# A hybrid encoder layer on one core: operands of the second half's input projection from x with channels on partitions

## The chip, the cores and the metric

The kernel runs on one core of a Trainium2 chip. The core has a matrix engine (TensorE, PE), three engines for element-wise work (VectorE or DVE, ScalarE or ACT, GpSimd or POOL), a queue engine that only issues transfers (SyncE, SP), and 16 DMA engines between the chip's memory and the on-chip SBUF. TensorE adds its products up in PSUM. The metric is the device time of one execution in microseconds; less is better. Several executions were timed, and one more was recorded by the hardware profiler.

## The reference

One layer with 2048 tokens and 1024 channels, all in float32. Cut to what matters here:

```python
xn = rmsnorm(x, norm1_g[l])          # x * rsqrt(mean(x*x) + 1e-6) * g
z = xn @ w_in[l]                     # the input projection, all columns
...
merged = gates[:, :, 0] * ya + gates[:, :, 1] * yb
x = x + merged @ w_o[l]
x = x + conv_glu_ffn(rmsnorm(x, norm2_g[l]), w_up[l], conv_w[l], conv_b[l], w_down[l])
...
return rmsnorm(x, final_g)
```

The change concerns the first two lines for the second half of the tokens: the normalised x is wanted with channels on partitions, since the matrix engine contracts over partitions.

## The kernel before

**Numbers.** A float32 operand is split into a high and a low part that the matrix engine takes at full rate (`split`, L680: the high part by ScalarE, L686, or GpSimd, L684; the low part, source minus high, by VectorE, L687). A product takes three matmuls of 128x512: high by high, high by low, low by high (`n_step`, L700).

**Seven products.** Large products run as a Strassen-like scheme: operands are cut into 2x2 blocks, and seven products P1 to P7 of sums of blocks replace eight. For x, the blocks are channels 0-511 or 512-1023 (four tiles of 128 channels each, k = 0..3 and 4..7) of one block of 512 tokens or the next: B11 and B21 from the first block, B12 and B22 from the second. The sums are T1 = B12 - B11, T2 = B22 - T1, T3 = B22 - B12 and T4 = B21 - T2 (up to the sign that the code keeps B22 with). Names such as `x_T20h` are the high part of T2, tile 0; `x_f0h` to `x_f7h` are those of B11 and B21.

**Stages.** The tokens are done in two halves of 1024, each of two blocks `b` of 512 (first half 0 and 1, second half 2 and 3); a block has four row tiles `j` of 128 tokens. Each half runs `mixer` and then `ffn`. `mixer` begins with `proj_io` (L1320), whose products come in the order P1, P2, P6, P5, ..., into the PSUM banks io_X, io_Y, io_Z, io_V: io_X uses B11, io_Y uses B21, the first io_Z uses T2, and io_V uses T1. `ffn` ends with the down-projection `down` (banks dn_P, L154 on PE as all matmuls with weights), in the order P1, P6, P2, P7, P5, P4, P3, each of 11 steps: a step takes one tile of weights and does 12 matmuls, three for each of four row tiles. So the end of the first half is dn P4, dn P3, and then the second half's io_X, io_Y, io_Z, io_V.

**Weights.** SP loads each tile of weights (`raw`, eight buffers, L203); ScalarE makes the high part (L250) and VectorE the low part (L251) in a ring of six (`ops`).

**Order.** Other work is written as tasks (generators) that are advanced a step every few matmuls; from what has been emitted, the framework's scheduler arranges the instructions by its own estimates, and each engine then runs its own list strictly in order. Working tiles come from one pool of 73 SBUF slots of 128x512 (`slot`).

**The forms of x, before.** `forms_of` (L935) makes two tasks. `forms_a_task` (L770) and `forms_b_task` (L819) first run `norm_rows` (L734) on the row tiles (`load_rows` loads them with tokens on partitions): ScalarE squares and sums a row (L727), GpSimd makes the root 1/sqrt(mean + eps) of each token (L730, L731), and VectorE scales the rows with it (`x_xs`, L744). TensorE then transposes 128x128 pieces into PSUM (`x_t`, L750), and ScalarE copies them out, times the gain (`x_b`, L758; with the sign turned, L850). The sums T1, T2, T3 are VectorE instructions that read PSUM (`minus`, L839), T4 is L891. For the second half, `forms_of` is called in `each3`, at step k = 1 (`X_AT`) of dn P3; the rows were loaded in dn P4 (`each4`). `go_io` keeps the second task from going on to transposes until `mixer` sets it.

**Beside it.** After dn P4 and dn P3 the first half's result gets its last normalisation (`final`): square sums `fj` on ScalarE (L1794), root on GpSimd (`fss`, L1852; `f_0r` and so on, L720 and L721), products `fo` on VectorE (L1861) or on ScalarE and GpSimd (L1858, L1859), and out. GpSimd's queue also fetches the operands of dn (`g_P`, L998), and SP loads `fg`, the last gain as one row for all partitions (L1900).

Of the kernel before, what the change touches and what calls it, by code (L numbers as in the profile page):

```python
# [11 lines left out]
F32 = mybir.dt.float32  # L12
F32R = mybir.dt.float32r
U8 = mybir.dt.uint8
AF = mybir.ActivationFunctionType
ALU = mybir.AluOpType
AX = mybir.AxisListType

P = 128
SEQ = 2048  # L20
D = 1024
KD = D // P
# [6 lines left out]
EPS = 1e-6  # L29
TB = 512  # L30
NT = TB // P
# [32 lines left out]
N_HEADS = 2  # L64
GO_AT = 3
LEAD = 5
X_AT = 1
WARM = 24, 5
GO_IO = (("P2", 1), ("P2", 0))
G_POOL = 4  # L70
# [11 lines left out]
LOOKAHEAD = 4  # L82
# [4 lines left out]
def tile_trunk(  # L87
    ctx: ExitStack,
    tc: tile.TileContext,
    x: bass.AP,  # L90
    w_in_t: bass.AP,
    w_io: bass.AP,
    pool_wt: bass.AP,
# [21 lines left out]
    def slot(name, cols=TB, dt=F32):  # L115
        return slots.tile([P, cols], dt, tag="s", name=name, padded_shape=[P, 528])
# [183 lines left out]
    stream = Stream()  # L300
# [271 lines left out]
    xt = {}  # L572
    ready = set()
# [9 lines left out]
    def load_rows(b):  # L583
        for j in range(NT):
            load_x_tile(b, j)
# [23 lines left out]
    def col(o):  # L609
        return cols[:, o : o + 1]  # L610
# [123 lines left out]
    def norm_rows(src, name, xs, after, lag=1):  # L734
        for j in range(NT):
# [9 lines left out]
                xs[j, hf] = t[hf]  # L745
            after(j)

    def transpose(ps, xs, j, k):
        c = (k % 4) * P
        return pe.transpose(ps[:, j * P : (j + 1) * P], xs[j, k // 4][:, c : c + P], ident)  # L750
# [184 lines left out]
    def forms_of(kind, b, gain, after=lambda b: lambda j: None, early=False, go=lambda: True):  # L935
        forms = {k: [] for k in ("B11", "B21", "B22", "T1", "T2", "T3", "T4", "task")}
        full = {k: [] for k in ("B11", "B21", "T2")}
        first = Task(forms_a_task((kind, b), gain, forms, full, after(b), early))
        forms["task"].append(first)
        late = Task(forms_b_task((kind, b + 1), gain, forms, full, after(b + 1), go, early))  # L940
        return forms, first, late

    def need(forms, key, late):
        task = forms["task"][0] if key in ("B11", "B21") else late
# [761 lines left out]
    def ffn(b0, forms, late):  # L1706
# [202 lines left out]
        def each3(k):  # L1909
            if k == 0:  # L1910
                down.make(len(down.steps))
            if k == X_AT and not last:
                nxt.append(forms_of("x", b0 + 2, o_n1, go=lambda: go_io[0]))

        def each4(k):
            if k in (0, 4) and not last:
                load_rows(b0 + 2 + k // 4)

        flush()
        down.run("P1", 0, each0)  # L1920
# [1 line left out]
        down.run("P2", 0, each1)  # L1922
        down.run("P7")
        down.run("P5", 0, each2)
        down.run("P4", 2, each4, lambda j: Task(final(0, j)))
        go_io[0] = False
        down.run("P3", 5 if last else 3, each3, lambda j: Task(final(1, j)), last)
        return nxt[0] if nxt else None

# [71 lines left out]
```

## Time and profile before

| | before |
|---|---|
| median of 3 timed executions | 2472.25 us (2472.08 to 2472.85) |
| the profiled execution | 2470.74 us |
| its span in the trace | 2468.7 us |
| granted TensorE clock | 1.0 |
| HBM traffic | 232 GB/s over the span |

The span is what the trace covers from the first to the last instruction; the execution's own time is 2 us longer. The page's rows with the most to do with the change are quoted in the prediction. Busy time is how long an engine worked; the chain of work that ended last is followed back from the last instruction, and says which engine's work set the end. A group's row gives the instructions of one line with their tiles, their count, busy time, mean length of one in ns, and how long the engine had idled before them. In the row of a window the brackets give the number of instructions.

### The profile page before, as it was taken

The numbers are of one execution on the slowest core, as the hardware profiler recorded it, in microseconds if no ns is written. First come the engines' busy times: TensorE is split into PE (matmuls) and PEld (weight loads), VectorE is DVE, ScalarE is ACT, GpSimd is POOL, SyncE is SP. The second block draws the span as 40 slices with busy tenths as digits, with TensorE's granted clock in tenths as the row PEclk, the third lists the DMA queues.
The fourth block names the chain that finished last, engine by engine and source line by source line (L and its number), as shares of the span: only waits on it lengthen the run. The fifth ranks groups of instructions, "written<-read, shape, count | busy, mean of one in ns | idle before, by whom it ended". The sixth has DMA issues, their size and how long they took to land.

```text
span 2468.7 us, 37997 instructions
## 1 busy us (share of the span) xinstructions
PE 2448.3 (99%) x12708; PEld 1986.6 (80%) x12708; DVE 1921.2 (78%) x3318; ACT 1237.0 (50%) x2376; POOL 783.6 (32%) x1090
## 2 busy tenths in 40 slices
PE   9999999999999999999999999999999999999998
PEld 7887877788888888888888888887888888888887
DVE  7777776897998778875586667769889987778755
ACT  6545544435555454553555455552465544445534
POOL 5343353403444333551330101123033332335310
PEclk9999999999999999999999999999999999999999
DMA  8889887777898779897444343456343444447852
GB/s 271 271 223 270 246 220 232 244 229 251 205 264 232 224 224 246 269 357 241 137 149 151 128 134 124 150 191 236 124 137 126 152 154 136 145 144 252 312 167 98
DMA packets 257699, 497.83 MB, mean 202 GB/s; under 512 B 26912, under 2 KB 47520, under 8 KB 257184
## 3 DMA queue, kind: packets, MB, share of 16 engines
q1 hardware_dynamic: 189872, 317.53, 38.9%
q0 software_dynamic: 42656, 112.74, 17.9%
q10 hardware_dynamic: 24976, 65.13, 7.6%
q8 instruction: 100, 1.64, 0.3%
q14 instruction: 95, 0.78, 0.1%
HBM read 383.63 MB, written 189.27 MB: 232 GB/s over the span
## 4 chain that ended last, share of the span: by engine, by line
PE 91%; DVE 4%; DMA 1%; issue 1%; ACT 1%; POOL 0%; SPq 0%; ACTq 0%; DVEq 0%; POOLq 0%
PE dn_P L154 17%; PE up_Z L154 15%; PE up_V L154 10%; PE up_X L154 10%; PE wo_P L154 6%; PE gr_V L154 3%; PE gr_X L154 3%; PE pb L154 3%; PE io_Z L154 3%; PE io_V L154 2%; PE gr_Z L154 2%; PE fr_V L154 1%; PE gr_W L154 1%; PE fr_X L154 1%; PE gr_Y L154 1%
## 5 line engine op out<-in xcount | busy, mean ns | idle before, releaser
L250 ACT CAST ops<-raw 128x512 fp32r<-128x512 f32 x792 | 487.1, 620 | 784.2 <-PE dn_P L154 175.2
L251 DVE TENSOR_TENSOR ops<-raw,ops 128x512 fp32r<-128x512 f32 x792 | 590.1, 749 | 238.8 <-ACT ops L250 226.6
L1735 DVE SCALAR_TENSOR_TENSOR e<-h,cols,e 128x512 f32<-128x512 f32 x176 | 143.0, 817 | 30.1 <-ACT e L1733 25.5
L1733 ACT ACTIVATE e<-h,cols 128x512 f32<-128x512 f32 x176 | 142.2, 814 | 25.2 <-DVE h L1183 18.7
L998 POOL DMA_DIRECT2D g_P<-dg_P x154 | 83.7, 545 | 173.7 <-PE dn_P L154 125.5
L1738 DVE SCALAR_TENSOR_TENSOR e<-h,cols,e 128x512 f32<-128x512 f32 x176 | 133.9, 770 | 2.5
L1304 POOL TENSOR_TENSOR gf_P<-e,e 128x512 f32<-128x512 f32 x44 | 61.6, 1402 | 149.4 <-DVE e L1744 89.4
L472 POOL TENSOR_TENSOR raw<-raw,raw 128x512 f32<-128x512 f32 x36 | 52.2, 1451 | 99.0 <-DVE ops L251 72.3
L1304 POOL TENSOR_TENSOR gf_P<-gf_P,e 128x512 f32<-128x512 f32 x44 | 58.4, 1328 | 74.0 <-DVE e L1744 71.7
L1728 POOL COPY h<-h 128x2 f32<-128x2 f32 x88 | 40.0, 466 | 107.3 <-DVE h L1182 99.6
L1742 ACT ACTIVATE e<-e 128x512 f32<-128x512 f32 x88 | 55.6, 632 | 35.1 <-DVE e L1738 34.8
L1183 DVE TENSOR_TENSOR h<-up_u,up_V 128x512 f32<-128x512 f32 x88 | 60.1, 683 | 10.4 <-PE up_V L154 9.9
L1730 POOL COPY hist<-h 128x2 f32<-128x2 f32 x88 | 35.2, 401 | 99.1 <-DVE h L1183 97.0
L1728 POOL COPY h<-hist 128x2 f32<-128x2 f32 x88 | 46.9, 539 | 53.8 <-ACT ops L250 35.5
L1444 POOL TENSOR_TENSOR q<-q,qs 128x512 f32<-128x512 f32 x16 | 22.3, 1397 | 122.2 <-ACT qs L1443 122.2
L1279 DVE TENSOR_TENSOR x<-x,wo_P 128x512 f32<-128x512 f32 x88 | 55.9, 681 | 6.2 <-PE wo_P L154 6.0
L1279 DVE TENSOR_TENSOR ac<-ac,dn_P 128x512 f32<-128x512 f32 x72 | 47.2, 681 | 12.3 <-PE dn_P L154 11.9
L1223 ACT COPY up_e<-up_X 128x512 f32<-128x512 f32 x44 | 25.8, 587 | 60.6 <-PE up_X L154 39.0
L1477 ACT ACTIVATE gt<-gt,cols 128x512 f32<-128x512 f32 x48 | 34.8, 725 | 42.1 <-DVE gt L1183 41.0
L1758 POOL DMA_DIRECT2D dg_P<-gf_P x88 | 50.7, 576 | 8.2 <-POOL gf_P L1304 7.4
L720 POOL TENSOR_SCALAR ro<-so 128x4 f32<-128x4 f32 x16 | 3.9, 244 | 147.6 <-ACT sq L1156 147.3
L1618 POOL TENSOR_TENSOR ya<-ya,gl 128x512 f32<-128x512 f32 x24 | 36.7, 1552 | 26.1 <-DVE ya L1615 17.6
(1326 smaller groups left out, 7916.1 us busy)
## 6 DMA issues: line engine op xcount, KB each, us to landing
g_P<-dg_P POOLq DMA_DIRECT2D x154, 256.0 KB, 5.7
raw<-in_w_up_t SPq DMA_DIRECT2D x132, 256.0 KB, 3.1
raw<-in_w_in_t SPq DMA_DIRECT2D x98, 256.0 KB, 3.6
dg_P<-gf_P POOLq DMA_DIRECT2D x88, 256.0 KB, 3.8
dg_P<-e SPq DMA_DIRECT2D x66, 256.0 KB, 3.3
raw<-in_w_dn SPq DMA_DIRECT2D x66, 256.0 KB, 3.6
x<-in_x SPq DMA_DIRECT2D x64, 256.0 KB, 4.8
gd<-gt ACTq DMA_DIRECT2D x64, 256.0 KB, 3.6
```

The source lines that it names most:

```text
L154: count[1] = pe.matmul(*args, **kw)
L250: self.mark = act.copy(hi, v)
L251: low = self.low = dve.tensor_tensor(lo, v, f32(hi), ALU.subtract)
L998: eng.dma_start(t, d)
L1183: return dve.tensor_tensor(dst, t, ps, ALU.add if how == "add" else ALU.subtract)
L1279: dve.tensor_tensor(t, t, ps[j], ALU.add if sg > 0 else ALU.subtract)
L1304: pin(eng.tensor_tensor(t, x0, x1, op))
L1728: pool.tensor_copy(h[:, 0:2], hist[:, mt] if hf == 0 else hs[s, 0][:, TB : TB + 2])
L1733: in_turn(act.activation(t, h[:, 2:], AF.Identity, bias=col(o_cb + mt), scale=col(o_cw + 4 * MF + mt)))
L1735: in_turn(second(dve.scalar_tensor_tensor(t, h[:, 1 : 1 + TB], col(o_cw + 2 * MF + mt), t, ALU.mult, ALU.add)))
L1738: dve.scalar_tensor_tensor(t, h[:, 0:TB], col(o_cw + mt), t, ALU.mult, ALU.add)
L1742: in_turn(act.activation(g, g, AF.Silu))
```

## The change

The kernel gets x a second time, as `x_ct`, its transpose: 1024 channels by 2048 tokens, laid out so on the host before the launch. For the second half (blocks 2 and 3) `channel_forms` replaces `forms_of("x", ...)`. A tile of channels is loaded as it stands (`xc`). Squares of the rows are still summed on ScalarE from the row tiles, but the four sums of a block become one 128x4 root on GpSimd, which is written to DRAM (`rx`, 512 elements of 4 bytes) and read back as one row of 512 tokens broadcast to all partitions (`x_rt`). `normed` is one VectorE instruction: channel tile times gain (one per partition) times root. The sums T1 to T4 are VectorE instructions on SBUF tiles. The tasks are now made at step 8 of dn P4 and not at step 1 of dn P3, and `go_io` is cleared before dn P4. The first half, and the forms of the up-projection, stay as they were.

```diff
-X_AT = 1
+X_AT = 8
...
+    def load_channels(b, k):
+        t = slot(f"xc{b}_{k}")
+        sp.dma_start(t, x_ct[k * P : (k + 1) * P, b * TB : (b + 1) * TB])
+        return t
+
+    def root_rows(b, name):
+        ss = small.tile([P, 2, 4], F32, tag="ssx", name=f"{name}ss")
+        for j in range(NT):
+            while (("x", b), j) not in ready:
+                yield 1
+            for c in range(2):
+                act.activation(slot(f"{name}xs{j}_{c}"), xt.pop((("x", b), j, c)), AF.Square,
+                               scale=1.0 / 32.0, accum_out=ss[:, c, j : j + 1])
+        r = small.tile([P, 4], F32, tag="rstd", name=f"{name}r")
+        pool.tensor_tensor(r, ss[:, 0], ss[:, 1], ALU.add)
+        pool.tensor_scalar(r, r, 1.0, EPS, ALU.mult, ALU.add)
+        pool.tensor_tensor(r, r, neghalf, ALU.pow)
+        d = dram.tile([NT, P], F32, tag=f"rx{b}", name=f"rx{b}")
+        pool.dma_start(d.rearrange("j p -> p j"), r)
+        t = slot(f"{name}rt")
+        pool.dma_start(t, d.rearrange("j p -> (j p)").partition_broadcast(P))
+        return t
+
+    def normed(xc, rt, c, name):
+        t = slot(name)
+        dve.scalar_tensor_tensor(t, xc, c, rt, ALU.mult, ALU.mult)
+        return t
+
+    def channels_a_task(b, gain, forms, full):
+        name = f"x{b}_"
+        xc = [load_channels(b, k) for k in range(4)]
+        rt = yield from root_rows(b, name)
+        yield 4
+        for k in range(KD):
+            key = "B11" if k < 4 else "B21"
+            t = normed(xc[k], rt, col(gain + k), f"{name}b{k}")
+            if k + 4 < KD:
+                xc.append(load_channels(b, k + 4))
+            yield 1
+            full[key].append(t)
+            forms[key].append(split(t, f"{name}f{k}", True))
+
+    def channels_b_task(b, gain, forms, full, go):
+        name = f"x{b}_"
+        xc = [load_channels(b, k) for k in (0, 4)]
+        rt = yield from root_rows(b, name)
+        yield 6
+        b12, b22, t1 = [], [], []
+        for k in range(4):
+            x12, x22 = xc[2 * k : 2 * k + 2]
+            if k < 3:
+                xc += [load_channels(b, i) for i in (k + 1, k + 5)]
+            b12.append(normed(x12, rt, col(gain + k), f"{name}c{k}"))
+            b22.append(normed(x22, rt, negs[:, gain + k + 4 : gain + k + 5], f"{name}b{k}"))
+            yield 3
+        while not go() or len(full["B21"]) < 4:
+            yield 1
+        for k in range(4):
+            t1.append(slot(f"{name}t1{k}"))
+            dve.tensor_tensor(t1[k], b12[k], full["B11"][k], ALU.subtract)
+            t2 = slot(f"{name}t2{k}")
+            dve.scalar_tensor_tensor(t2, b22[k], -1.0, t1[k], ALU.mult, ALU.subtract)
+            forms["T2"].append(split(t2, f"{name}T2{k}"))
+            full["T2"].append(t2)
+            yield 1
+        for k in range(4):
+            forms["T1"].append(split(t1[k], f"{name}T1{k}"))
+            yield 4
+        for k in range(4):
+            dve.tensor_tensor(b12[k], b12[k], b22[k], ALU.add)
+            forms["T3"].append(split(b12[k], f"{name}T3{k}"))
+            yield 1
+        for k in range(4):
+            t4 = slot(f"{name}t4{k}")
+            dve.tensor_tensor(t4, full["B21"][k], full["T2"][k], ALU.subtract)
+            forms["T4"].append(split(t4, f"{name}T4{k}"))
+            forms["B22"].append(split(b22[k], f"{name}B22{k}"))
+            yield 1
+        stream.room = LOOKAHEAD
...
+    def channel_forms(b, gain, go):
+        forms = {k: [] for k in ("B11", "B21", "B22", "T1", "T2", "T3", "T4", "task")}
+        full = {k: [] for k in ("B11", "B21", "T2")}
+        first = Task(channels_a_task(b, gain, forms, full))
+        forms["task"].append(first)
+        return forms, first, Task(channels_b_task(b + 1, gain, forms, full, go))
 
...
         def each3(k):
             if k == 0:
                 down.make(len(down.steps))
-            if k == X_AT and not last:
-                nxt.append(forms_of("x", b0 + 2, o_n1, go=lambda: go_io[0]))
 
         def each4(k):
             if k in (0, 4) and not last:
                 load_rows(b0 + 2 + k // 4)
+            if k == X_AT and not last:
+                nxt.append(channel_forms(b0 + 2, o_n1, lambda: go_io[0]))
 
         flush()
         down.run("P1", 0, each0)
@@ -1922,8 +2010,8 @@
         down.run("P2", 0, each1)
         down.run("P7")
         down.run("P5", 0, each2)
+        go_io[0] = False
         down.run("P4", 2, each4, lambda j: Task(final(0, j)))
-        go_io[0] = False
         down.run("P3", 5 if last else 3, each3, lambda j: Task(final(1, j)), last)
         return nxt[0] if nxt else None
 
...
     feed = {
         "x": a["x"][0],
+        "x_ct": a["x"][0].T,
```

Lines move by up to 89 in the changed kernel: L154 becomes L155, L251 L252, L687 L688, L1279 L1367, L1861 L1949. What stands in each engine's list, place by place:

VectorE, where the operands of the first io_Z are made (`fo` is the last normalisation of the first half; `ops` a weight's low part; `x_t_...<-x_t_...,cols,x_b` the sums that read PSUM). Before:

```order
L1861 SCALAR_TENSOR_TENSOR fo_1_3_0_13044<-ac_1_3_0_11560,f_1_3r,fg_0_12011 128x512
L1861 SCALAR_TENSOR_TENSOR fo_1_3_1_13045<-ac_1_3_1_10964,f_1_3r,fg_1_12013 128x512
L839 SCALAR_TENSOR_TENSOR x_t_13116<-x_t_13104,cols,x_b_12801 128x512
L839 SCALAR_TENSOR_TENSOR x_t_13118<-x_t_13109,cols,x_t_13116 128x512
L839 SCALAR_TENSOR_TENSOR x_t_13120<-x_t_13104,cols,x_b_13114 128x512
L687 TENSOR_TENSOR x_T20l<-x_t_13118,x_T20h 128x512
L839 SCALAR_TENSOR_TENSOR x_t_13144<-x_t_13132,cols,x_b_12818 128x512
L839 SCALAR_TENSOR_TENSOR x_t_13146<-x_t_13137,cols,x_t_13144 128x512
L839 SCALAR_TENSOR_TENSOR x_t_13148<-x_t_13132,cols,x_b_13142 128x512
L251 TENSOR_TENSOR ops_13221<-raw_12852,ops_13221 128x512
L687 TENSOR_TENSOR x_T21l<-x_t_13146,x_T21h 128x512
```

The same place in the changed kernel (L808 makes t1, L810 t2, L818 T3):

```order
L1949 SCALAR_TENSOR_TENSOR fo_1_2_0_12990<-ac_1_2_0_11558,f_1_2r,fg_0_12011 128x512
L1949 SCALAR_TENSOR_TENSOR fo_1_2_1_12991<-ac_1_2_1_10962,f_1_2r,fg_1_12013 128x512
L1949 SCALAR_TENSOR_TENSOR fo_1_3_0_13022<-ac_1_3_0_11560,f_1_3r,fg_0_12011 128x512
L1949 SCALAR_TENSOR_TENSOR fo_1_3_1_13023<-ac_1_3_1_10964,f_1_3r,fg_1_12013 128x512
L808 TENSOR_TENSOR x_t_13082<-x_c_12690,x_b_12602 128x512
L252 TENSOR_TENSOR ops_13110<-raw_12877,ops_13110 128x512
L252 TENSOR_TENSOR ops_13143<-raw_12889,ops_13143 128x512
L810 SCALAR_TENSOR_TENSOR x_t_13084<-x_b_12692,x_t_13082 128x512
L818 TENSOR_TENSOR x_c_12690<-x_c_12690,x_b_12692 128x512
L252 TENSOR_TENSOR ops_13167<-raw_12946,ops_13167 128x512
L688 TENSOR_TENSOR x_T20l<-x_t_13084,x_T20h 128x512
```

The three sums of one k were three instructions reading PSUM, and are now three on SBUF tiles; low parts of weights stand between them. The normalised tiles `x_b` and `x_c` that they read were made further up in the same list.

TensorE, at the step from io_Y to the first io_Z. Before:

```order
L154 MATMUL io_Y_13094<-ops_13068,x_f7h 128x512 x2
L154 MATMUL io_Y_13094<-ops_13068,x_f7l 128x512
L750 MATMUL x_t_13193<-ident,x_xs_0_12639 128x128
L750 MATMUL x_t_13193<-ident,x_xs_0_12649 128x128
L750 MATMUL x_t_13193<-ident,x_xs_0_12659 128x128
L750 MATMUL x_t_13193<-ident,x_xs_0_12669 128x128
L750 MATMUL x_t_13198<-ident,x_xs_1_12640 128x128
L750 MATMUL x_t_13198<-ident,x_xs_1_12650 128x128
L750 MATMUL x_t_13198<-ident,x_xs_1_12660 128x128
L750 MATMUL x_t_13198<-ident,x_xs_1_12670 128x128
L154 MATMUL io_Z_13267<-ops_13099,x_T20h 128x512 x2
L154 MATMUL io_Z_13267<-ops_13099,x_T20l 128x512
```

In the changed kernel:

```order
L155 MATMUL io_Y_13072<-ops_13046,x_f7h 128x512 x2
L155 MATMUL io_Y_13072<-ops_13046,x_f7l 128x512
L155 MATMUL io_Z_13189<-ops_13077,x_T20h 128x512 x2
L155 MATMUL io_Z_13190<-ops_13077,x_T20h 128x512 x2
L155 MATMUL io_Z_13191<-ops_13077,x_T20h 128x512
L155 MATMUL io_Z_13189<-ops_13077,x_T20l 128x512
L155 MATMUL io_Z_13190<-ops_13077,x_T20l 128x512
L155 MATMUL io_Z_13191<-ops_13077,x_T20h 128x512
```

The eight transposes between them are gone, as are the other 56 of blocks 2 and 3. The matmuls of io_Z now go through the four row tiles with one operand (T2's tile 0) before the next.

GpSimd, from the last fetches for dn P3 to the first half's last normalisation. Before:

```order
L998 DMA g_P_8_12448<-dg_P_8_10225 128x512
L1852 TENSOR_TENSOR fss_0_0_12475<-fss_0_0_12475 128x1
L720 TENSOR_SCALAR f_0_0r<-fss_0_0_12475 128x1
L721 TENSOR_TENSOR f_0_0r<-f_0_0r,neghalf 128x1
L1852 TENSOR_TENSOR fss_0_1_12493<-fss_0_1_12493 128x1
L998 DMA g_P_9_12525<-dg_P_9_10575 128x512
L720 TENSOR_SCALAR f_0_1r<-fss_0_1_12493 128x1
L721 TENSOR_TENSOR f_0_1r<-f_0_1r,neghalf 128x1
```

In the changed kernel (L763 to L765 the roots of a block, L767 their way to DRAM, L769 their broadcast back):

```order
L1086 DMA g_P_8_12448<-dg_P_8_10225 128x512
L763 TENSOR_TENSOR x_r<-x_ss 128x4
L764 TENSOR_SCALAR x_r<-x_r 128x4
L765 TENSOR_TENSOR x_r<-x_r,neghalf 128x4
L767 DMA rx_12492<-x_r 128x4x1
L769 DMA x_rt<-rx_12492 128x512
L763 TENSOR_TENSOR x_r<-x_ss 128x4
L764 TENSOR_SCALAR x_r<-x_r 128x4
L765 TENSOR_TENSOR x_r<-x_r,neghalf 128x4
L767 DMA rx_12521<-x_r 128x4x1
L769 DMA x_rt<-rx_12521 128x512
L1940 TENSOR_TENSOR fss_0_0_12537<-fss_0_0_12537 128x1
```

Two chains of three small operations and two transfers now stand ahead of `fss_0_0`; both transfers of a block are issued from this queue, the second after the first has landed.

SP, after the weights of the first io_Z have been asked for (`kw...ioP` are sums of weights kept in DRAM by the first half):

```order
L204 DMA raw_12860<-kw0ioP_485 128x512
L204 DMA raw_12877<-kw1ioP_502 128x512
L751 DMA xc_2_12747<-in_x_ct 128x512
L751 DMA xc_6_12749<-in_x_ct 128x512
L204 DMA raw_12889<-kw2ioP_571 128x512
L204 DMA raw_12946<-kw3ioP_642 128x512
L751 DMA xc_3_12799<-in_x_ct 128x512
L751 DMA xc_7_12801<-in_x_ct 128x512
```

The loads of block 3's last channel tiles stand behind the weights' loads in this queue.

More of the change, by code (lines that the diff above doesn't have):

```diff
@@ L90, in tile_trunk @@
     x: bass.AP,
+    x_ct: bass.AP,
     w_in_t: bass.AP,
```

## The prediction

> **What bounds the kernel now.** I read the page's busy line first, then the chain that ended last, then the same chain in the stretch that the change touches.
>
> ```profile
> PE 2448.3 (99%) x12708; PEld 1986.6 (80%) x12708; DVE 1921.2 (78%) x3318; ACT 1237.0 (50%) x2376; POOL 783.6 (32%) x1090
> PE 91%; DVE 4%; DMA 1%; issue 1%; ACT 1%; POOL 0%; SPq 0%; ACTq 0%; DVEq 0%; POOLq 0%
> by line: PE dn_P L154 44.4%; PE io_Z L154 15.5%; PE io_V L154 11.2%; PE io_Y L154 11.1%; PE io_X L154 11.1%; PE x_t L750 7.0%
> ...
> 1245.90 1.75 PE x_t L750 x16
> 1247.64 11.10 PE io_X L154 x48
> ...
> 1273.35 11.14 PE io_Z L154 x48
> 1284.50 11.18 PE io_V L154 x48
> ```
>
> The third line is the chain from 1200 to 1300 us, where the first half's down-projection ends and the second half's input projection begins. Nothing but TensorE is on it. The transposes of x are 7.0% of 100 us, so 7.0 us; 16 in 1.75 us make 0.109 us each, and 64 of them 7.0 us. A step of 48 matmuls is 11.1 us, 0.232 each.
>
> ```profile
> core 0: us, PE busy (x) PEld busy (x) DVE busy (x) ACT busy (x) POOL busy (x), PEclk, DMA share, GB/s
> 1216.00:1230.00 14.00, 14.00 (x62) 11.38 (x61) 14.00 (x16) 13.50 (x34) 11.13 (x13) 1.00 0.57 188
> 1272.00:1286.00 14.00, 14.00 (x67) 11.41 (x66) 13.71 (x23) 7.20 (x13) 0.00 (x0) 1.00 0.55 187
> 1209.00:1278.00 69.00, 69.00 (x333) 56.79 (x332) 60.30 (x90) 50.14 (x118) 38.95 (x54) 1.00 0.46 153
> ```
>
> TensorE is busy in all 69 us, at full clock, so the whole gain must come from TensorE work that goes. VectorE is the next engine: 60.30 of 69 us, and all of 1216 to 1230. That is the cover to watch.
>
> **The change, part by part.**
>
> *TensorE.* All 64 transposes (L750) of blocks 2 and 3 go: 32 ahead of io_X, 32 within io_Y. If nothing is late, io_X starts 3.5 us earlier, at 1244.1, and io_Z 7.0 us earlier, at 1266.3. **Term: −7.0 us.**
>
> *ScalarE* loses 12 copies out of PSUM; its 16 squares move forward, into P4.
>
> ```profile
> L758 ACT ACTIVATE x_b<-x_t,cols x12: 675/690/725, 15.6 to 1252.6; 128x512 f32<-128x512 f32 x12
> L850 ACT ACTIVATE x_b<-x_t,negs x8: 681/686/701, 33.3 to 1273.6; 128x512 f32<-128x512 f32 x8
> 1185.77 0.62 ACT L250 CAST ops<-raw 128x512 fp32r<-128x512 f32 x1 [2.13 <-PE dn_P L154]
> 1199.61 0.62 ACT L250 CAST ops<-raw 128x512 fp32r<-128x512 f32 x1 [2.17 <-PE dn_P L154]
> ...
> 1210.10 0.63 ACT L1794 ACTIVATE fj<-ac 128x512 f32<-128x512 f32 x1 [1.50 <-DVE ac L1279]
> ```
>
> Eight L758 and four L850 are 8.3 us off an engine that has room. In the new order the squares of block 2 stand around the cast of 1185.77 (one before it, seven behind) and six of block 3 ahead of the cast of 1199.61. Between casts ScalarE idles 2.1 us, so seven squares (0.63 us, as the square fj, and some 0.1 for reading its sum) push one cast back by some 3 us. The ring of weights is six deep and each is used for 12 matmuls (2.78 us), so I put this at nothing; without that cover it would cost up to the 3 us.
>
> *VectorE* decides. Up to the split T23l, the last operand that io_Z waits for, the order of before has 103 instructions from the last accumulations of P4 (L1279, near 1209 us) on, that of the changed kernel 104. Gone are 16 scalings x_xs (L744) and 12 subtractions that read PSUM (L839). New are 16 normalizing products and four t2 (the same instruction as fo, L1861), eight sums of two SBUF tiles (the form of L687), and one weight rest (L251) that now comes ahead.
>
> ```profile
> L251 DVE TENSOR_TENSOR ops<-raw,ops 128x512 fp32r<-128x512 f32 x22 | 19.3, 900 | 2.1 <-ACT ops L250 2.1
> L839 DVE SCALAR_TENSOR_TENSOR x_t<-x_t,cols,x_b 128x512 f32<-128x512 f32 x8 | 5.9, 742 | 0.0
> L744 DVE TENSOR_SCALAR x_xs<-x,x_2r 128x512 f32<-128x512 f32 x4 | 1.8, 490 | 1.2 <-POOL x_2r L731 1.2
> L744 DVE TENSOR_SCALAR x_xs<-x,x_1r 128x512 f32<-128x512 f32 x4 | 1.8, 499 | 1.2 <-POOL x_1r L731 1.2
> L744 DVE TENSOR_SCALAR x_xs<-x,x_3r 128x512 f32<-128x512 f32 x4 | 1.8, 492 | 0.7 <-POOL x_3r L731 0.7
> L744 DVE TENSOR_SCALAR x_xs<-x,x_0r 128x512 f32<-128x512 f32 x4 | 1.8, 481 | 0.5 <-POOL x_0r L731 0.5
> L687 DVE TENSOR_TENSOR x_f7l<-x_b,x_f7h 128x512 fp32r<-128x512 f32 x1 | 0.7, 693 | 0.5 <-POOL x_f7h L684 0.5
> ...
> 1215.93 0.75 DVE L1861 SCALAR_TENSOR_TENSOR fo<-ac,f_0r,fg 128x512 f32<-128x512 f32 x1
> 1216.59 0.74 DVE L1861 SCALAR_TENSOR_TENSOR fo<-ac,f_1r,fg 128x512 f32<-128x512 f32 x1
> 1217.26 3.66 DVE L251 TENSOR_TENSOR ops<-raw,ops 128x512 fp32r<-128x512 f32 x1
> 1222.65 0.67 DVE L687 TENSOR_TENSOR dn_P_6l<-g_P,dn_P_6h 128x512 fp32r<-128x512 f32 x1
> 1223.26 0.67 DVE L687 TENSOR_TENSOR dn_P_7l<-g_P,dn_P_7h 128x512 fp32r<-128x512 f32 x1
> ```
>
> Instructions overlap at their ends, so I count starts: fo follows fo after 0.66 us, a split a split after 0.61. Gone: 4 × 1.8 = 7.2, and 12 × 0.66 = 7.9, together 15.1 us. New: 20 × 0.66 = 13.2, and 9 × 0.61 = 5.5, together 18.7. Work: +3.6 us. With the x_xs go their waits for roots, 0.5 + 1.2 + 1.2 + 0.7 = 3.6 us. Other waits in the stretch (f_r, x_f7h, first splits), some 2.2 us, shrink as VectorE has more queued; I take them as gone, and bound them by staying. New waits come for splits that VectorE queues close behind their high half and for channel tiles of block 3 that SP issues late: one or two of the sizes in the rows above (0.5 to 1.2), 0.6 to 1.5, taken as 1.2. So T23 shifts by 3.6 − 3.6 − 2.2 + 1.2 = **−1.0 us**, bounds −1.6 and +1.5.
>
> ```profile
> 1281.56 1.56 PE L154 MATMUL io_Z<-ops,x_T23h 128*128 128x512 f32 x6
> ...
> 1276.47 0.62 ACT L686 CAST x_T23h<-x_t 128x512 fp32r<-128x512 f32 x1 [2.18 <-DVE x_t L839]
> ...
> 1277.13 0.69 DVE L687 TENSOR_TENSOR x_T23l<-x_t,x_T23h 128x512 fp32r<-128x512 f32 x1
> ```
>
> The high half of T23 is ready at 1277.1 now and first used at 1281.56: a cover of 4.5 us. TensorE comes 7.0 us earlier, at 1274.6, the operand at 1276.1: **a stall of 1.5 us**, between 0.9 and 4.0 by those bounds. T20 to T22 wait for the same queue; their lateness is contained in it, not added. What follows (T1, T3, T4 and io_V) has the same delay behind it and finds its operands just in time. Term: **+1.5 us**.
>
> *GpSimd and DMA.* Sixteen tiny root operations become six, and two pairs of DMAs come: the roots to DRAM (512 elements of 4 bytes), and back as one row broadcast over partitions. SP issues 16 more loads of 256 KB, 4.2 MB in some 60 us, 70 GB/s on top of the 153 in this stretch. The page's slices show up to 357 GB/s, so I cost the bytes at nothing; if these loads held the weights up beyond the ring of eight raw tiles, they would cost TensorE what exceeds it.
>
> ```profile
> GB/s 271 271 223 270 246 220 232 244 229 251 205 264 232 224 224 246 269 357 241 137 149 151 128 134 124 150 191 236 124 137 126 152 154 136 145 144 252 312 167 98
> ...
> 1211.53 0.19 POOL L1852 TENSOR_TENSOR fss<-fss 128x1 f32<-128x1 f32 x1 [33.27 <-ACT fj L1794]
> ...
> 1212.08 0.56 POOL L721 TENSOR_TENSOR f_0r<-f_0r,neghalf 128x1 f32<-128x1 f32 x1
> ...
> L1900 SPq DMA_DIRECT2D fg<-in_final_g x4: 333/384/467, 1112.7 to 2302.3; - x4
> ...
> DMA to landing us min/median/max: 5.6/6.9/8.2
> ...
> vd<-v SPq DMA_DIRECT2D x4, 256.0 KB, 2.2
> ```
>
> The nearest row for the broadcast is fg, a row spread over all partitions in the same way: its line gives a median of 6.9 us to landing. No row has the writing of single elements; I bound it by 2.2 (vd, a tile to DRAM) and 6.9 and take the middle, 4.5, since it has few bytes but many pieces. Block 2's squares end near 1191.4, three GpSimd steps add some 1.1 (as fss and f_0r, 1211.53 to 1212.64), the pair of DMAs 11.4: the roots are there at 1203.9. VectorE reaches the first product near 1216, so 12 us are spare. GpSimd waits in order for the first DMA before it issues the second: for block 3 (squares until about 1201.7) until 1207.3, and it is next needed at 1211.53, so 4.2 us are spare there. **Cost: nothing**, with these two covers.
>
> The Trainium skill speaks against this route: its page "DMA: Bandwidth & Descriptors", Specifications, says that transfers below 512 bytes make the DMA engines read, modify and write. No run here shows what 512 four-byte pieces then take; with the cover above it would change the sum only by becoming the last rival below.
>
> **Sum.** −7.0 + 1.5 = −5.5 us: the profiled execution's 2470.74 (span 2468.7) becomes 2465.2. The median of the runs is 2472.25, 1.5 us above that execution; there the forecast is **2466.8 us** (−0.22%). The stall's bounds, 0.9 and 4.0, make 2466.2 to 2469.3.
>
> **The rivals.**
>
> *A. Nothing is late.* If VectorE loses its waits and meets no new ones (shift −2.2 or better), the stall is at most 0.3 us: 2465.3 to 2465.8. For it: TensorE waits nowhere in this stretch now. Against it: VectorE has 60 of 69 us of work already.
>
> *B. VectorE becomes the bound.* For it speaks the row of 1217.26: a weight rest of 3.66 us instead of 0.67 while GpSimd multiplies two tiles of fo.
>
> ```profile
> 1217.66 1.32 POOL L1859 TENSOR_TENSOR fo<-fo,fg 128x512 f32<-128x512 f32 x1
> ...
> 1219.06 1.30 POOL L1859 TENSOR_TENSOR fo<-fo,fg 128x512 f32<-128x512 f32 x1
> ```
>
> Twelve operations that read PSUM (L839, 742 ns each, so not stretched) go and 28 that read two SBUF tiles come, in the time in which GpSimd splits x and scales fo. Two more collisions of 1.3 us, or one as long as that of 1217.26 (3.0 more), raise the stall to 4.1 to 4.5, and with the upper bound of the waits to 7.0: 2469.4 to 2472.2, within 0.2% of before. The Trainium skill has the rule in "GPSIMD Engine Reference", 1. Specifications: GpSimd shares its SBUF interfaces with VectorE, and VectorE instructions with two SBUF inputs contend. The row of 1217.26 agrees. By that rule all 28 are open to it; I hold it to few, since GpSimd's heavy work (11.13 of 14 us) lies in 1216 to 1230 and VectorE is stretched there already.
>
> *C. The roots come too late, and it is slower than before.* The mechanism is the first DMA of a pair. If it takes 17.5 us and not 4.5, GpSimd is held until 1220.3, 8.8 us beyond its need; about 3.3 of that is covered, since the first fo on VectorE starts at 1215.93, and the other 5.5 us reach TensorE through VectorE's queue and take the gain away. At 22.5 us the kernel is 5 us slower than before, 2477. For it: nothing like 512 single elements is in the trace. Against it: every row of a DMA in this stretch is under 7 us.
>
> *D. The transposes don't go.* The order of the changed kernel has none of them between the two halves, so this gets no chance.
>
> **How the numbers follow.** Forecast (stall 0.5 to 2.5 us, 2465.8 to 2467.8) 40%; A 22%; B with the upper part of the waits (2467.8 to 2472.2) 27%; C 11%. The measurement tells about 0.2% from no change, 4.9 us, so faster is below 2467.3: all of A and four fifths of the forecast, 54%. Within 0.2%: the rest of the forecast, B, and the part of C that stays below 2477.2, together 39%. Slower: 7%. The range goes from the full gain with half a microsecond of luck, 2464.8, to the upper end of B, 2472.0; it leaves C out and little else.
>
> **What would show it.** In the changed kernel's trace io_X should start near 1244.1 and io_Z near 1266.3 to 1267. TensorE should wait 0.9 to 4 us at io_Z's first operands T20 to T23, released by ScalarE's high halves or VectorE's T2 splits. VectorE should have no idle above 1.5 us at the products. GpSimd's first fss after the roots should still start at 1211.5. No wait of TensorE at all would say A; stretched products beside GpSimd's fo and x_f high halves would say B; products idle for the roots would say C. A wait for weights (raw, SP's queue) anywhere here would show a cost that I put at nothing.

## The result and the profile after

| | before | changed | ratio (95%) |
|---|---|---|---|
| median of 14 and 14 executions | 2472.09 us | 2467.30 us | 0.998 (0.9973 to 0.9987) |
| the same, with other kernels of the study (28 and 11) | 2471.11 us | 2467.58 us | 0.999 (0.9981 to 0.9998) |
| the profiled execution, its span | 2470.74, 2468.7 us | 2467.66, 2465.9 us | |

The forecast was 2466.8 us, in a range from 2464.8 to 2472.0. Of the two intervals, 3.2 to 6.7 us and 0.5 to 4.7 us were gained. That is the whole run; the trace shows what the boundary itself gained, and it was less than forecast. For that a mark is needed on each side of the boundary. I take two casts of weights on ScalarE: the one between the splits of dn_P_6 and dn_P_7, ahead of dn P4, and one in the gr stage, some 80 us after io_V has begun. From the timeline of ScalarE, the kernel before (start, length):

```profile
1146.88 0.62 ACT L250 CAST ops<-raw 128x512 fp32r<-128x512 f32 x1 [1.61 <-PE dn_P L154]
...
1365.00 0.61 ACT L250 CAST ops<-raw 128x512 fp32r<-128x512 f32 x1
```

and the same two casts of the changed kernel:

```profile
1149.07 0.62 ACT L251 CAST ops<-raw 128x512 fp32r<-128x512 f32 x1 [1.61 <-PE dn_P L155]
...
1364.26 0.61 ACT L251 CAST ops<-raw 128x512 fp32r<-128x512 f32 x1
```

From cast to cast it was 218.12 us and is 215.19 us: **2.93 us gained at the boundary**, where 5.5 were forecast. The difference from 7.0 lies in waits of TensorE that were not there before. The page's busy line and chain, and the view of TensorE's waits from 1100 to 1340 us (engine, line, releaser: us in total, times, longest), changed kernel:

```profile
PE 2441.9 (99%) x12644; PEld 1979.5 (80%) x12644; DVE 1923.3 (78%) x3318; ACT 1229.8 (50%) x2364; POOL 777.6 (32%) x1084
PE 88%; DVE 6%; DMA 2%; issue 2%; ACT 1%; POOL 1%; SPq 0%; ACTq 0%; DVEq 0%; POOLq 0%
...
PE dn_P L155 <- DVE ops L252: 0.8, 1, 0.8
PE dn_P L155 <- DVE dn_P_5l L688: 0.7, 1, 0.7
PE io_Z L155 <- ACT x_T23h L687: 0.6, 1, 0.6
PE io_Z L155 <- ACT x_T20h L687: 0.4, 1, 0.4
```

Exactly 64 matmul instructions are gone from TensorE (12708 to 12644). The four rows are 2.5 us. Counted from start to start of the matmuls, against the usual 0.232 us, six stalls with the slower matmul behind each take 4.2 us: 2.0 in dn P3, 2.2 in the four steps of io_Z. And −7.0 + 4.2 = −2.8 is what the casts show. Where they come from is seen on the other engines. The windows that were shown of before, and one between them (busy time of each engine, clock, DMA share, GB/s):

```profile
core 0: us, PE busy (x) PEld busy (x) DVE busy (x) ACT busy (x) POOL busy (x), PEclk, DMA share, GB/s
1216.00:1230.00 14.00, 14.00 (x61) 11.09 (x59) 9.09 (x12) 8.72 (x20) 11.59 (x19) 1.00 0.60 186
1230.00:1244.00 14.00, 12.53 (x54) 9.87 (x54) 13.77 (x18) 4.65 (x8) 5.78 (x5) 1.00 0.71 240
1272.00:1286.00 14.00, 13.27 (x56) 9.91 (x55) 13.85 (x23) 7.66 (x15) 0.00 (x0) 1.00 0.45 161
1209.00:1278.00 69.00, 66.97 (x285) 52.81 (x284) 58.80 (x85) 33.36 (x73) 28.38 (x40) 1.00 0.62 197
```

From 1216 to 1230 VectorE was busy for all 14 us before, and now for 9.09. It idles there although it has more to do than before. The timeline of GpSimd says why:

```profile
1195.70 0.83 POOL L767 DMA_DIRECT2D rx<-x_r  x1 [0.29 <-POOL x_r L765]
1204.17 0.56 POOL L769 DMA_DIRECT2D x_rt<-rx  x1 [7.64 <-DMA rx<-x_r]
...
1208.23 0.82 POOL L767 DMA_DIRECT2D rx<-x_r  x1 [1.41 <-issue]
1217.69 0.57 POOL L769 DMA_DIRECT2D x_rt<-rx  x1 [8.64 <-DMA rx<-x_r]
1218.28 0.63 POOL L1940 TENSOR_TENSOR fss<-fss 128x1 f32<-128x1 f32 x1
```

and the timeline of VectorE just behind (in brackets the idle time ahead, and what ended it):

```profile
1219.88 0.75 DVE L1949 SCALAR_TENSOR_TENSOR fo<-ac,f_0r,fg 128x512 f32<-128x512 f32 x1 [1.02 <-POOL f_0r L722]
1220.55 0.68 DVE L252 TENSOR_TENSOR ops<-raw,ops 128x512 fp32r<-128x512 f32 x1
1222.37 0.69 DVE L252 TENSOR_TENSOR ops<-raw,ops 128x512 fp32r<-128x512 f32 x1 [1.14 <-ACT ops L251]
1225.36 0.69 DVE L688 TENSOR_TENSOR x_f0l<-x_b,x_f0h 128x512 fp32r<-128x512 f32 x1 [2.30 <-POOL x_f0h L685]
```

The roots' write to DRAM takes 8.5 and 9.5 us from its issue to the next instruction on GpSimd. GpSimd stands until 1217.69, fss_0_0 begins at 1218.28, and VectorE, whose queue is in order, waits for f_0r, for a cast (ScalarE's product fo ahead of it waits for f_0r too, 1.88 us) and for x_f0h, which GpSimd makes behind fss and the roots: 4.5 us in these rows. (These times are not to be laid beside those of before as they stand: the first mark is 2.19 us later in this trace, so 1217.69 here is 1215.50 there.)

### The profile page after: what moved, and what is told of

Its sections match the earlier page's. It is cut to its first block, busy times and chain, and to the rows that moved or that the text cites. A ratio compares the mean times of both kernels' runs of the same rounds, so it can differ in the third digit from the quotient of the medians.

```text
span 2465.9 us, 37864 instructions
## 1 busy us (share of the span) xinstructions
PE 2441.9 (99%) x12644; PEld 1979.5 (80%) x12644; DVE 1923.3 (78%) x3318; ACT 1229.8 (50%) x2364; POOL 777.6 (32%) x1084
## 4 chain that ended last, share of the span: by engine, by line
PE 88%; DVE 6%; DMA 2%; issue 2%; ACT 1%; POOL 1%; SPq 0%; ACTq 0%; DVEq 0%; POOLq 0%
PE dn_P L155 17%; PE up_Z L155 15%; PE up_V L155 10%; PE up_X L155 10%; PE wo_P L155 4%; PE gr_V L155 3%; PE gr_X L155 3%; PE io_Z L155 2%; PE pb L155 2%; PE io_V L155 2%; PE gr_W L155 2%; PE gr_Y L155 1%; PE fr_X L155 1%; PE gr_Z L155 1%; DVE ops L252 1%
## 5 line engine op out<-in xcount | busy, mean ns | idle before, releaser
L251 ACT CAST ops<-raw 128x512 fp32r<-128x512 f32 x792 | 487.3, 620 | 770.3 <-PE dn_P L155 167.0
L252 DVE TENSOR_TENSOR ops<-raw,ops 128x512 fp32r<-128x512 f32 x792 | 587.0, 745 | 236.1 <-ACT ops L251 226.7
L1367 DVE TENSOR_TENSOR x<-x,wo_P 128x512 f32<-128x512 f32 x88 | 55.8, 677 | 5.7 <-PE wo_P L155 5.4
L1367 DVE TENSOR_TENSOR ac<-ac,dn_P 128x512 f32<-128x512 f32 x72 | 47.2, 681 | 11.9 <-PE dn_P L155 11.5
```

The lines of the kernel that those rows point to most:

```text
L251: self.mark = act.copy(hi, v)
L252: low = self.low = dve.tensor_tensor(lo, v, f32(hi), ALU.subtract)
L1367: dve.tensor_tensor(t, t, ps[j], ALU.add if sg > 0 else ALU.subtract)
```

## Experiments

Two theories are set against each other. **H**: GpSimd, held by the roots' DMA, makes VectorE late, and the waits come from that. **V**: the volume of VectorE's work ahead of T2 makes io_Z wait, whatever GpSimd does. In this table "cast to cast" is the stretch between the two marks, "T23l" is the end of that split counted from the first mark, "waits" is TensorE's stall from 1180 to 1310 us counted from start to start as above, and "median" is that of the timed executions against before in the same set.

| run | cast to cast, against 218.12 | waits, us | T23l, us | median against before (95% of the ratio) |
|---|---|---|---|---|
| before, two traces | 0, +0.01 | none | 130.9 | |
| changed, two traces | −2.93, −2.95 | 4.2, 4.1 | 132.3 | −4.8 (0.9973 to 0.9987), −3.5 (0.9981 to 0.9998) |
| pe_back | +1.45 | 1.4 | 131.3 | +0.7 (0.9994 to 1.0011) |
| rx16 | −5.90 | 1.2 | 129.4 | −7.3 (0.9962 to 0.9983) |
| t3late | −2.04 | 4.8 | 130.7 | −6.0 (0.9966 to 0.9985) |
| xat4 | −0.14 | 6.8 | 129.8 | −1.7 (0.9982 to 1.0) |
| xat7 | −5.92 | 1.3 | 127.8 | −6.9 (0.996 to 0.9982) |
| rows4 | −5.69 | 1.4 | 129.5 | −5.8 (0.9966 to 0.9985) |
| rows4_t3 | −5.51 | 1.6 | 127.6 | −6.6 (0.9963 to 0.9986) |
| rows4_xat6 | −5.22 | 1.8 | 125.5 | −4.7 (0.9971 to 0.9988) |
| rows4_xat7 | −7.11 | none | 125.7 | −9.2 (0.9951 to 0.9979) |
| rows4_fin24 | −0.80 | 5.9 | 123.1 | −2.1 (0.9986 to 1.0003) |

In every row the second column is −7.0 plus the waits, to within 0.3 us (for pe_back, which has the 64 instructions back, the waits alone). So the books at the boundary close: TensorE's instructions and its waits, and nothing else.

**The transposes' worth (pe_back).** Undone is only TensorE's part:

```diff
             t = normed(xc[k], rt, col(gain + k), f"{name}b{k}")
+            warm(4)
...
         for k in range(4):
+            warm(8)
             t1.append(slot(f"{name}t1{k}"))
```

> 64 transposes of the identity are put back on TensorE (32 in dn P3 beside the products of block 2, 32 beside T2), with no other work added; their results are not used. The TensorE part alone: 64 x 0.109 = 7.0 us come back. They cover what io_Z waits for (2.3 us), so the time rises by 4.5 to 5.5 us against the changed kernel, to about that of before. If the gain had come from the other engines (copies and squares off ScalarE, PSUM reads off VectorE), it would rise by under 3 us.

Cast to cast rose by 4.4 us against the changed kernel, just under the 4.5 to 5.5 that were expected, and the median returned to that of before (ratio 1.0002). io_Z no longer waits; what is left:

```profile
PE io_X L155 <- DVE ops L252: 0.6, 1, 0.6
PE dn_P L155 <- DVE ops L252: 0.3, 1, 0.3
```

So the gain is TensorE's 64 instructions; they were also the cover under which late operands went unseen.

**The DMA's pieces (rx16).** The same instructions and bytes, with 128 pieces of 16 bytes:

```diff
-        d = dram.tile([NT, P], F32, tag=f"rx{b}", name=f"rx{b}")
-        pool.dma_start(d.rearrange("j p -> p j"), r)
+        d = dram.tile([P, NT], F32, tag=f"rx{b}", name=f"rx{b}")
+        pool.dma_start(d, r)
...
-        pool.dma_start(t, d.rearrange("j p -> (j p)").partition_broadcast(P))
+        pool.dma_start(t, d.rearrange("p j -> (p j)").partition_broadcast(P))
```

> The roots go to DRAM as 128 pieces of 16 bytes instead of 512 pieces of 4 bytes, and are read back in that order, so each token gets another token's root; all instructions and sizes stay the same. Theory H (GpSimd, held by the first DMA until 1217.7 us, makes VectorE late): that DMA takes at most 4 us instead of 8.5, GpSimd is free for fss by 1213.5, the two waits in dn P3 (1.9 us with what follows them) go, the four waits of the first io_Z (2.3 us) shrink to under 1, and the time falls by 2.5 to 3.5 us against the changed kernel. Theory V (the volume of VectorE's work ahead of T2 makes io_Z wait): the waits of io_Z stay near 2.3 us whatever GpSimd does; at most the 1.9 us in dn P3 go. If the price is the round trip and not the pieces, the DMA stays over 7 us and nothing moves.

The DMA views from 1150 to 1300 us (KB each, median us from issue to landing), first of the changed kernel:

```profile
x_rt<-rx POOLq DMA_DIRECT2D x2, 256.0 KB, 4.3
rx<-x_r POOLq DMA_DIRECT2D x2, 2.0 KB, 8.4
```

then of rx16, with its first fss from GpSimd's timeline and its only wait of TensorE:

```profile
rx<-x_r POOLq DMA_DIRECT2D x2, 2.0 KB, 2.8
...
1212.93 0.19 POOL L1940 TENSOR_TENSOR fss<-fss 128x1 f32<-128x1 f32 x1 [3.60 <-ACT fj L1882]
...
PE io_Z L155 <- ACT x_T23h L687: 0.6, 1, 0.6
```

2.8 us instead of 8.4 for the same 2 KB. GpSimd is now idle ahead of fss and waits for ScalarE, as in the kernel before; both waits in dn P3 are gone, and T23l ends 3.0 us earlier. That is theory H, for 3.0 of the 4.2 us. What is left, 1.2 us in io_Z, is neither's by this run.

**The same with the right result (rows4).** The row tiles of these blocks serve only the square sums, so their rows may lie in any order. With the lines of rx16:

```diff
+        rows = x[b * TB : (b + 1) * TB].rearrange("(p j) c -> p j c", j=NT)
...
+                sp.dma_start(t, rows[:, j, 512 * c : 512 * c + 512])
```

> The row tiles of blocks 2 and 3, of which only the square sums are used, are loaded with token 4p+j on partition p of tile j instead of token 128j+p, so that the roots go to DRAM as 128 pieces of 16 bytes in token order. Theory H: as in the run with the roots in the wrong order: the first DMA takes 2.8 us and not 8.4, no wait in dn P3, 1.2 us of waits in io_Z; 2.5 to 3 us under the changed kernel. If only the order of the run before made it fast, or the other loading of rows costs, it is not under the changed kernel.

It came out as rx16: the DMA took 3.0 us, the waits 1.4, cast to cast −5.69. The other way of loading the rows costs nothing that can be seen.

**The volume ahead of T2 (t3late, rows4_t3, rows4_fin24).** First the four sums T3, which stand among T20 to T23 on VectorE but are needed later, are put behind T23l:

```diff
+            t2_low = last_split[0][1]
...
-            dve.tensor_tensor(b12[k], b12[k], b22[k], ALU.add)
+            ins = dve.tensor_tensor(b12[k], b12[k], b22[k], ALU.add)
+            behind(ins, t2_low)
```

> The four sums T3 are ordered behind the split T23l on VectorE; nothing else is moved by hand. Theory V: four instructions of 0.6 us leave the queue ahead of T23l, so T21, T22 and T23 come 0.6, 1.8 and 2.4 us earlier, the four waits of io_Z (2.3 us) shrink to 0.6 (T20's), and the time falls by 1.5 to 2 us. Theory H alone, with VectorE waiting for others between its instructions there: less than 0.7 us falls, since VectorE then idles instead. Both: the waits in dn P3 stay at 1.9 us.

T23l came 1.6 us earlier and the waits for T21 to T23 were gone. But there are new ones:

```profile
PE io_V L155 <- DVE v L1273: 1.2, 1, 1.2
...
PE io_Z L155 <- DVE io_u L1440: 0.6, 1, 0.6
PE io_Z L155 <- ACT x_T20h L687: 0.5, 1, 0.5
```

The sums now stand ahead of `v` and `io_u`, with which VectorE frees PSUM banks for io_V and the next io_Z. In all 0.9 us were lost at the boundary (the median, −6.0, does not show it). I had expected 1.5 to 2 us of gain. With the short DMA and the sums behind T13l instead (`t1_low`, taken in the loop over T1):

```diff
+            t1_low = last_split[0][1]
...
-            dve.tensor_tensor(b12[k], b12[k], b22[k], ALU.add)
+            ins = dve.tensor_tensor(b12[k], b12[k], b22[k], ALU.add)
+            behind(ins, t1_low)
```

> As the run with rows loaded four apart, and the four sums T3 ordered behind the split T13l on VectorE. Theory V for what is left: the 1.2 us of waits in io_Z come from the volume of work ahead of T23l, so they go, and no wait of over 0.5 us comes in their place; 0.7 to 1.2 us faster than without the reordering, all of the 7.0 us gained. Rival: as where T3 stood right behind T23l, the wait moves to io_V or the product after it (T3 late), and nothing is gained.

The waits in io_Z were gone, and one of 1.4 us for `io_u` came in their place: the rival. And with eight products fo of the last normalisation moved behind T13l, on top of rows4:

```diff
-FIN_WAIT = 4
+FIN_WAIT = 28
```

> As the run with rows loaded four apart, and the last normalisation of block 1 begins 24 steps later (FIN_WAIT 28), so that its eight products fo (some 5 us of VectorE) stand behind the split T13l and not ahead of T20. Theory V for the rest: VectorE reaches T20 to T23 some 5 us earlier, no wait is left in io_Z, and if the products fo then fit beside io_V, the whole 7.0 us are gained (local gain 6.5 to 7). Rival: VectorE has no free room after T23 either, the wait comes back in io_V or the product behind it, and the local gain stays at 5.7 or below.

T23l came 6.5 us earlier, no wait was left up to io_V, and then TensorE stood for `io_u`:

```profile
PE io_Z L155 <- DVE io_u L1447: 3.5, 1, 3.5
```

Again the rival, and worse. VectorE has little room up to the second io_Z (here it is busy for 13.29 of the 14 us from 1272 on and 12.50 of the next 14), and what is put back there only stands ahead of something else. Theory V holds for the rest of the waits; delaying VectorE's work does not cure them.

**When the tasks begin (xat4, xat7, rows4_xat6, rows4_xat7).** `X_AT` alone, 4 instead of 8 (the other three differ in this line in the same way):

```diff
-X_AT = 8
+X_AT = 4
```

> X_AT is 4 instead of 8, so the tasks of the second half's operands begin four steps (11 us) earlier in dn P4. Both theories: the roots are back before the last normalisation needs GpSimd, VectorE makes more products ahead of 1216 us, no wait in dn P3, io_Z waits under 1 us in all; gain 6 to 7 us against before instead of the 4.8 measured. If slots or SP's queue are short so early, weights (raw) come late in P4 instead and the gain is 4 us or less.

This failed. io_Z has no wait, but dn P3 has three. TensorE's waits, and two rows of GpSimd's timeline, one of VectorE's and one of ScalarE's:

```profile
PE dn_P L155 <- ACT dn_P_4h L687: 1.8, 1, 1.8
PE dn_P L155 <- DVE dn_P_4l L688: 1.6, 1, 1.6
PE dn_P L155 <- DVE dn_P_5l L688: 1.4, 1, 1.4
...
1207.65 0.56 POOL L769 DMA_DIRECT2D x_rt<-rx  x1 [11.09 <-PE dn_P L155]
1209.30 0.64 POOL L685 TENSOR_SCALAR x_f0h<-x_b 128x512 fp32r<-128x512 f32 x1
...
1209.97 0.69 DVE L688 TENSOR_TENSOR x_f0l<-x_b,x_f0h 128x512 fp32r<-128x512 f32 x1 [10.17 <-POOL x_f0h L685]
...
1224.94 0.64 ACT L1882 ACTIVATE fj<-ac 128x512 f32<-128x512 f32 x1 [11.98 <-DMA xc<-in_x_ct]
```

On GpSimd the chain of roots of block 3 now stands ahead of x_f0h and of fetches of g_P, and holds it for 11.09 us ahead of the second x_rt. (The name in the bracket is the last event by the profile; the write itself landed at 1207.13.) VectorE has already come to x_f0l and stands for 10.17 us. It is late from there on: the first sum ac of dn P4's end starts at 1224.23 (the changed kernel: 1211.57, with a first mark 2.17 us earlier), and ScalarE, idle for 11.98 us ahead of fj, which reads that sum, reaches the split dn_P_4h only at 1230.20. The fetches of g_P that GpSimd issued right behind its hold had landed by 1214.44, so they are not what dn P3 waited for. With the short DMA:

> As the run with rows loaded four apart, with X_AT 6: the tasks begin two steps (5.6 us) earlier. Theory H and V: GpSimd's chain is over before it must fetch for dn P3, and VectorE makes some products before 1216 us, so no wait above 0.5 us is left: 6.5 to 7 us under before. Rival: what made X_AT 4 slow with the 4-byte roots (6.8 us of waits for the operands dn_P_4 and dn_P_5) is the early start itself and not the DMA's length; then waits of 2 us or more in dn P3 remain.

One wait of 1.5 us for dn_P_5l is left in dn P3. GpSimd is back from its DMAs at 1201.8 us there; the split stands on VectorE behind products of both blocks that were made earlier, two of them stretched to 1.82 and 1.10 us. Between the two starts:

> As the run with rows loaded four apart, with X_AT 7: between the start with 1.4 us of waits in io_Z (X_AT 8) and that with 1.8 us in dn P3 (X_AT 6). Theory V: VectorE's queue decides both, so the waits lie between or are moved from io_Z to dn P3, 0.5 to 1.8 us in all; local gain 5.2 to 6.5.

No wait of TensorE is left at all. Its chain from 1200 to 1300 us (start, length):

```profile
1199.80 44.62 PE dn_P L155 x192
1244.42 11.08 PE io_X L155 x48
1255.50 11.03 PE io_Y L155 x48
1266.54 11.07 PE io_Z L155 x48
1277.61 11.11 PE io_V L155 x48
```

The whole 7.0 us are gained (7.11 cast to cast); the median of 2462.34 us, 0.9965 (0.9951 to 0.9979) of before in five executions, is the lowest of the study, and 5 us below that of the changed kernel in another set; 2.1 of its 9.2 us are not from the boundary. I had expected 0.5 to 1.8 us of waits to be left. Last, `X_AT` 7 with the 4-byte pieces:

> X_AT 7 alone, with the roots in 4-byte pieces as in the changed kernel. Theory H, that the DMA counts only where GpSimd is needed before it lands: the chain of roots starts 6 to 7 us earlier on GpSimd, whose second hold ends near 1208 instead of 1217.7, ahead of the first fss (1212); so the waits in dn P3 are under 0.5 us and those in io_Z under 1, and the local gain is 6 us or more though the DMA still takes over 8 us. If the 16-byte pieces were needed, 2 us or more of waits in dn P3 remain, as with X_AT 4.

Partly right: the local gain is 5.9 us and io_Z does not wait, but dn P3 waits 1.3 us, and the hold ends at 1214.59, not 1208. The second write held GpSimd for nearly 12 us here:

```profile
1202.74 0.82 POOL L767 DMA_DIRECT2D rx<-x_r  x1 [0.30 <-POOL x_r L765]
1214.59 0.57 POOL L769 DMA_DIRECT2D x_rt<-rx  x1 [11.04 <-PE dn_P L155]
```

**What the stages elsewhere add (changed_again, before_again).**

> The changed kernel once more, beside the others of this set. Waits of TensorE at the boundary 4.2 us as in the first trace (1.9 in dn P3, 2.3 in io_Z with what follows each), the median 4 to 5.5 us under before.

> The kernel before once more, for a second trace of it. At the boundary it has no wait of TensorE, as in the first; the stages that the change does not touch differ by up to 2 or 3 us from one execution to another, as the first half's do between the traces taken so far. If those stages are as quick as in its first trace (1.4 to 2.8 us quicker in the first half than in eight traces of other kernels), the change would cost time there.

Cast to cast both repeated to 0.02 us, and their waits at the boundary came out as expected (4.1 us, none); the changed kernel's median, 3.5 us under before, was expected at 4 to 5.5. The first mark stood at 1146.88 in the first trace of before and at 1149.07 in the second, and between 1147.11 and 1151.24 in the others, so what is ahead of it differs from one execution to another by itself. From the second mark to the end it was 1103.7 and 1103.0 us in the traces of before, and 1100.3 to 1102.8, in the mean 1102.0, in the twelve others. That could be a gain of 1 us that belongs to the change, or the spread of two traces against twelve (the second traces of the two kernels, 1103.0 and 1102.8, differ by 0.2); it stays open.

## Why the prediction was right, point by point

The total lay 0.5 us from the forecast, but not for all the reasons given, and in part by luck.

- **TensorE, −7.0 us: right.** The 64 instructions put back alone bring the time of before back to within 1.5 us (pe_back), and where no wait is left (rows4_xat7) 7.1 us are gained. io_X was forecast at 1244.1 and io_Z at 1266.3; in that run, whose first mark lies 0.23 us later than that of before, they start at 1244.42 and 1266.54.
- **VectorE, T23 shifted by −1.0 us (bounds −1.6 and +1.5): right where GpSimd is not held.** rx16 has −1.6, rows4 −1.4. Its parts are right there too: from the first sum ac (1209.38 before) to the end of T23l VectorE is busy for 59.8 us before and 62.7 in rx16, 2.9 more (forecast 3.6), and idle for 8.6 and 4.2, 4.5 less (forecast 4.6). In the changed kernel it is busy for 61.4 and idle for 8.4: the idle time that was to go was there again, in other places. So the shift is +1.4, at the upper bound, and the cause is not the one for which that bound was set.
- **io_Z stalls by 1.5 us: the size was nearly right** (2.2 us in the changed kernel, 1.2 without the hold). T20 to T23 each wait some, and as the forecast had it, what they sum to is the lateness of T23: in the changed kernel the first matmul with T23h would have come 8.6 us (37 times 0.232) behind io_Y's last at 1270.08, and came at 1280.74, 2.1 us later, as soon as its cast had ended (1280.69).
- **"Cost: nothing" for GpSimd and DMA: wrong, and this is the step that failed.** The write of single elements was put at 4.5 us between 2.2 and 6.9. It took 8.4 and more, outside both ends; the rows that gave those move long pieces, and rx16 shows that the pieces make the price. The cover ahead of fss was 4.2 us. GpSimd came back 8.2 us later than forecast (1215.50 on the clock of before, not 1207.3). Of this, 5.0 are the second write (9.5 instead of 4.5), and 1.4 came because the first pair still held GpSimd when block 3's squares were done (1203.3, and its roots began at 1204.75); the rest is in the root steps and a pause of 1.41 us ahead of the write. The excess held GpSimd and then VectorE, and cost 2.0 us in dn P3 and 1.0 in io_Z, 3.0 in all (changed against rx16). That is the mechanism of rival C, short of the 17.5 us at which it would have taken the gain away; the forecast had it as all or nothing, and it came in part. Rival C's own cover was too wide as well. GpSimd was 4.0 us beyond its need of 1211.53; less the 3.3 us counted as covered, that would have cost 0.7 and not 3.0. The 3.3 us were those of the first fo alone, while x_f0h and a cast, which wait in the same queues, had less. The broadcast back was put at 6.9 us and took 4.3. The rule of the Trainium skill that was named beside it ("DMA: Bandwidth & Descriptors", Specifications: below 512 bytes the engines read, modify and write) does not give this price by itself: pieces of 16 bytes are below it too, and took 2.8 us.
- **Rival B, contention with GpSimd: it did not grow.** Of the 16 products, eight (block 2's) took 737 to 747 ns, and the longest of the others 1098:

```profile
L774 DVE SCALAR_TENSOR_TENSOR x_b<-xc,cols,x_rt x8: 737/742/747, 1218.1 to 1254.0; 128x512 f32<-128x512 f32 x8
L774 DVE SCALAR_TENSOR_TENSOR x_c<-xc,cols,x_rt x4: 739/740/1098, 1237.2 to 1259.6; 128x512 f32<-128x512 f32 x4
```

  They have two inputs in SBUF, so by the rule of the Trainium skill ("GPSIMD Engine Reference", 1. Specifications) all may contend. The trace agrees as far as it can: 13 of the 16 ran beside no operation of GpSimd on whole tiles, and of the three that did, the two that began after it were stretched (1092 and 1098 ns). Over all of VectorE's instructions from 1209.38 to T23l, what those of over 0.85 us took beyond 0.70 sums to 6.6 us before, 5.0 in the changed kernel and 6.5 in rx16.
- **ScalarE and the bytes of SP, nothing: right.** From 1180 us, ahead of the squares, to the middle of dn P3 TensorE does not wait in any run with X_AT 7 or 8, and its later waits for weights (`ops`) end with VectorE's low part.
- **The median: near for a lesser reason.** The boundary gained 2.9 us, not 5.5. The medians moved by 4.8 and 3.5, and only the second interval (0.5 to 4.7) holds 2.9. So the nearness of 2466.8 to 2467.3 is in part luck: what the stages elsewhere added, which no run here explains.
- **Two slips, of no consequence.** From the first ac at 1209.38 to T23l the traces have 88 and 89 instructions of VectorE, not 103 and 104; the difference, on which the term rests, is the same. A's stall of at most 0.3 us gives up to 2465.6, not 2465.8.

## What to carry to other kernels

An operation that is taken off the bounding engine takes its cover along: look at what the engine would wait for next, queue by queue, and where that queue is nearly full, start the work earlier, not later, but not so early that it stands ahead of what is due sooner (with the short write, one step earlier removed the waits here; two steps, and four with the long write, brought others). A transfer whose landing the same engine's queue waits for costs that engine the whole latency, so it belongs where the engine has nothing due; here 128 pieces of 16 bytes held it far less than 512 of 4. A local gain is read from two marks around the stage, which here repeat to 0.02 us where the medians' intervals are 3.5 to 6.9 us wide.

## What was not expected of the hardware

- The write of 2 KB from GpSimd's queue took 8.2 to 9.9 us (medians of six traces) as 512 pieces of 4 bytes and 2.8 to 3.7 us as 128 pieces of 16 (six traces). The number of pieces and their size changed together, so which of them counts was not told apart.
- A wait of 3.5 us cost more than its length. In rows4_fin24 TensorE stood from 1302.09 to 1305.59, and the windows from there on (columns as above) show the granted clock:

```profile
1301.00:1304.00 3.00, 1.09 (x5) 0.56 (x3) 2.92 (x5) 2.12 (x4) 0.00 (x0) 1.00 0.27 87
1304.00:1307.00 3.00, 1.41 (x3) 1.16 (x4) 2.93 (x6) 0.67 (x2) 0.00 (x0) 0.50 0.28 90
1307.00:1310.00 3.00, 3.00 (x9) 2.31 (x8) 2.93 (x5) 1.26 (x2) 0.00 (x0) 0.50 0.46 175
1310.00:1313.00 3.00, 3.00 (x13) 2.40 (x12) 0.83 (x2) 1.26 (x2) 0.00 (x0) 0.86 0.46 175
```

  It is 0.50 from 1304 on, still within the wait, and into the last of these windows. The matmuls then start 0.43 us apart instead of 0.232: of the 5.9 us lost, 2.2 are these slower matmuls. The Trainium skill ("TensorE: Matmul & The Clock Gate", Part 1) says that the clock is gated to half after an idle window of about 3.4 us. The trace agrees on the half, but not on so long an idle time: the clock was down some 1.9 us after the last matmul. And in xat4, where no wait was longer than 1.8 us, it fell as well, behind those of 1.8 and 1.6 us with two matmuls between them:

```profile
1230.00:1244.00 14.00, 10.15 (x36) 7.63 (x37) 13.49 (x18) 11.27 (x24) 11.47 (x15) 0.88 0.79 246
```

  The matmuls at half clock make some 1.2 of the 6.8 us lost there. Single waits of 1.4 to 1.5 us (rows4_t3, rows4_xat6) left the clock at 1.00, and so did those of the changed kernel, at most 0.8 us.
